# adaLN chunks with one 128-column block per column group and one transpose, and the first layer's gate chunks at the merge stage

## The chip, the core and the metric

The kernel runs on one core of one Trainium2 chip. The metric is the device time of one execution in microseconds (us).

## What is computed

One inference step of a trunk of two layers (`DEPTH` = 2), for 512 prompt positions and 8 single-position samples, 520 columns in all, with `D_MODEL` = 1024. Each layer is conditioned by adaLN: a small vector c (one row for the prompt, one for each of the 8 samples, so 9 rows) is multiplied by a 1024 x 3072 matrix, which gives shift, scale and gate. Cut to what matters:

```
mod = silu(c) @ w_ada + b_ada                  # 9 rows x 3072
shift, scale, gate = split(mod, 3)
h = rmsnorm(x) * (1 + scale) + shift           # needs shift and scale
proj = h @ w_in                                # seven projections of h
y_m = mlstm branch(proj);  y_c = convolution branch(proj)
merged = sigmoid(gm) * y_m + sigmoid(gc) * y_c
x = x + gate * (merged @ w_out)                # the gate is needed only here
```

Shift and scale are needed before the first projection of a layer, the gate only in its last product.

## The kernel before

Activations are held transposed, channels on the 128 partitions and the 520 columns along the free dimension, in tiles of 8 channel blocks (`KT` = 8). Every large product is done to nearly full float32 precision with three fast products (high x high, high x low, low x high): `split_w` loads a 128 x 1024 weight tile `raw` (L167, SP's queue), ACT rounds it to `whi` (L173), GpSimd subtracts to get `wlo` (L176), and `dense` (L188) multiplies, 48 matmuls of 128 x 260 for a block of 128 output channels. `raw` has two buffers and `whi`/`wlo` three, so the weights are prepared a few blocks ahead.

The adaLN matrix of a layer is cut into 6 chunks of 512 columns (`w_ada[l, c]`, 2 MB each in 4 transfers, L275): chunks 0 to 3 hold scale and shift, each for two channel blocks of h; chunks 4 and 5 hold the gate. One chunk goes like this. `ada_mul` (L292) multiplies the 32-column tile `cT[:, k]` (9 of its columns are c, the others zero) as weights with the chunk's 512 columns, for the 8 blocks k of the contraction. Block k writes to partitions 32(k mod 4) and up, so that four blocks in a row use the four column groups of TensorE, and the four groups hold four partial sums. ACT copies the 128 x 512 result to `asb` (L294). The `tail` (L300) then has four matmuls with 128 columns of `asb` as weights and the selector `sel32` as the other operand: this turns the block round and adds the four partial sums. DVE adds the bias into `mod` (L301), and for chunks 0 to 3 makes `sa` = (1 + scale) * norm weight (L306).

Where the chunks stand: in layer 0, chunks 0 to 3 are loaded in the prologue behind x. The first dense product is `dense_pair` (L248), a loop over the contraction that can start on the first blocks of h while the later ones are still being made: its `hook` does chunk c = 1, 2, 3 after block k = 1, 3, 5, and then makes the two blocks `hh`/`hl` of h that this chunk gives (`norm_in`, L433 to L452). After `gab(0)`, the first convolution input, come chunks 4 and 5 of layer 0, loaded into the tiles that later hold q and v; then `do_xm`, `do_v` and `do_qk` for the four heads. Layer 1's chunk 0 is loaded into the tile `xc` and multiplied in layer 0's merge stage (the loop over m that makes `mrg`, two dense products a turn) after m = 3; chunk 1 follows in the next stage; chunks 2 to 5 are done at the boundary of the layers.

The 31-tap convolution is done on DVE, tap by tap (L515), in tasks that `fill(n)` hands out between the dense products. The order of instructions on each engine is set by the framework's scheduler, which plays the program through with its own times; where an instruction stands in an engine's queue is fixed from then on. An engine that waits holds up all behind it.

Of the kernel before, what the change touches and what calls it, by code (L numbers as in the profile page):

```python
# [11 lines left out]
F32 = mybir.dt.float32  # L12
# [8 lines left out]
L = 2  # L21
D = 1024
KT = D // 128
# [52 lines left out]
def build(nc, tc, ctx, ap):  # L76
# [8 lines left out]
    sml = pool("sml")  # L85
# [3 lines left out]
    v, s, g, te = nc.vector, nc.scalar, nc.gpsimd, nc.tensor  # L89

    ident = const.tile([128, 128], F32, name="ident")
    make_identity(nc, ident)
    sel32 = const.tile([128, 32], F32, name="sel32")
# [43 lines left out]
    class Pairs:  # L137
# [7 lines left out]
        def tail(self, i, n):  # L145
            return self.tiles[i][:, :, T - n:T]

    def t520(name):
        return tmp.tile([128, T], F32, tag="t520", bufs=T5B, name=name)
# [81 lines left out]
    cT = const.tile([128, KT, 32], F32, name="cT")  # L231
# [28 lines left out]
    def ada_start(l):  # L260
        avec = sml.tile([128, 32], F32, tag="avec", bufs=2, name="avec")
        nc.sync.dma_start(avec, ap["avec"][l])
        mod = sml.tile([128, 24, 9], F32, tag="mod", bufs=2, name="mod")
        sa = sml.tile([128, KT, 9], F32, tag="sa", bufs=2, name="sa")
        return avec, mod, sa
# [11 lines left out]
    def ada_load(l, c, tag):  # L277
        raw = ada_tile(tag)
        for kp in range(0, 4, 2):
            ada_half(l, c, raw, kp)  # L280
        return raw

    def ada_chunk(l, adas, c, tag, ps=("m", 3)):
        return ada_mul(adas, c, ada_load(l, c, tag), ps)

    def ada_mul(adas, c, raw, ps=("m", 3), stream=False):
        vec, mod, sa = adas
        acc = pm("ada", *ps)
        for n in range(KT):
            k = n if stream else KT - 1 - n  # L290
            r = 32 * (k % 4)
            te.matmul(acc[r:r + 32, :], cT[:, k, :], raw[k // 2][:, k % 2, :], start=(n < 4), stop=(n >= 4))  # L292
        asb = t520("asb")
        s.copy(asb[:, 0:512], acc)  # L294

        def tail():
            pt = pm("adat", *ps)
            ks = slice(c * 4, c * 4 + 4)
            for i in range(4):
                te.matmul(pt[:, i * 9:i * 9 + 9], asb[:, i * 128:(i + 1) * 128], sel32[:, 0:9], start=True, stop=True)  # L300
            v.tensor_tensor(out=mod[:, ks, :], in0=pt[:, 0:36].rearrange("p (m r) -> p m r", r=9),  # L301
                            in1=vec[:, O_BADA + c * 4:O_BADA + c * 4 + 4].unsqueeze(2).to_broadcast([128, 4, 9]),
                            op=ALU.add)
            if c < 4:
                o = 2 * c
                v.scalar_tensor_tensor(out=sa[:, o:o + 2, :], in0=mod[:, 4 * c:4 * c + 2, :], scalar=1.0,  # L306
                                       in1=vec[:, O_NORM + o:O_NORM + o + 2].unsqueeze(2).to_broadcast([128, 2, 9]),
                                       op0=ALU.add, op1=ALU.mult)
        return tail
# [96 lines left out]
    acc = sum_sq(x)  # L406
    x_src = ap["x"]
    adas = ada_start(0)

    for l in range(L):  # L410
        avec, mod, sa = adas
# [210 lines left out]
            return proj(tuple(a[:, 512:1024] for a in w), xcs, kk, h, DH ** -0.5)  # L622

        gab(0, w=w01)
        if l == 0:
            gtails = [ada_chunk(l, adas, 4, "q"), ada_chunk(l, adas, 5, "v")]
        else:
            gtails.append(ada_mul(adas, *raws.pop(0)))
        for tail in gtails:
            tail()  # L630
        xc = big.tile([128, KT, T], F32, tag="xc", name="xc")
        q = big.tile([128, KT, T], F32, tag="q", name="q")
        kk = Pairs("k", F32, "kk")
# [2 lines left out]
        for h in range(H):  # L636
# [6 lines left out]
            mm = do_qk(h)  # L643
# [14 lines left out]
        with tc.issue_after(mm.ins):  # L658
            for r in range(6):
                for n, c in enumerate(HALF):  # L660
                    for j in range(4):
                        t, k = srcs[r * 4 + j]
                        o = O_WG + (t * 8 + k) * 8
                        te.matmul(pgs[n][32 * j:32 * j + 32, 0:HT], vec[:, o:o + 32], (q, kk, vv)[t][:, k, c],  # L664
                                  start=(r == 0), stop=(r == 5))
# [40 lines left out]
        mm = gab(2, raw=True)  # L706
        pt = pm("pst")
# [9 lines left out]
        for j in range(2):  # L717
            for h in range(H):
                te.matmul(pv_[32 * h:32 * h + 32, j * 128:(j + 1) * 128], vv[:, 2 * h + j, T - 32:T], ident,
                          start=True, stop=True)  # L720
# [4 lines left out]
        for j in range(2):  # L725
            for h in range(H):
                te.matmul(pv_[32 * h:32 * h + 32, 256:258], prod[:, 2 * h + j, :], ones[:, 0:2],
                          start=(j == 0), stop=(j == 1))
# [228 lines left out]
        mm = gab(7)  # L957
        pt = pm("pths")
# [4 lines left out]
        for j in range(2):  # L963
            v.tensor_tensor(
                out=hsm[:, :, j, :],
                in0=pt[:, j * 128:(j + 1) * 128].rearrange("p (h c) -> p h c", h=H)[:, :, S0:32],
# [6 lines left out]
        for m0 in range(0, KT, 2):  # L973
            ws = split_w(ap["wst"][l, PR_ZM + m0 // 2], 2)
            for j in range(2):
                m = m0 + j
# [31 lines left out]

        mrg = Pairs("v", F32, "mrg")
        if l + 1 < L:  # L1010
            adas = ada_start(l + 1)
            raw = ada_load(l + 1, 0, "xc")
        for m in range(KT):
            wg, wb = split_w(ap["wst"][l, PR_GMB + m], 2)
            sg = t520("sgm")
            dense(wg, hh, hl, KT, lambda c, p: s.activation(sg[:, c], p, AF.Sigmoid))

            def ev(c, p):
                i = v.tensor_tensor(out=mrg[:, m, c], in0=p, in1=sg[:, c], op=ALU.mult)
                with tc.issue_after(i.ins):  # L1020
                    fill(F_GM)

            mm = dense(wb, hmh, hml, KT, ev)
            if l + 1 < L and m == 3:
                with tc.issue_after(mm.ins):
                    tail = ada_mul(adas, 0, raw)

        sgc = Pairs("k", F32, "sgc")
        if l + 1 < L:
            tail()  # L1030
            tail = ada_chunk(l + 1, adas, 1, "q")
# [14 lines left out]
        for m0 in range(0, KT, 2):  # L1046
            ws = split_w(ap["wst"][l, PR_ZC + m0 // 2], 2)
            for j in range(2):
                m = m0 + j
# [151 lines left out]
```

## Time and profile before

| | |
|---|---|
| median of 3 runs | 1283.85 us (1280.69 to 1285.78) |
| the profiled execution | 1279.5 us, its span 1277.8 us |
| TensorE matmul (PE) busy | 1226.5 us, 96% of the span |
| VectorE (DVE), GpSimd (POOL), ScalarE (ACT) busy | 843.3, 682.4, 531.8 us |
| DMA | 177.14 MB, mean 139 GB/s |
| adaLN matmuls (L292) | 192 records for 96 matmuls, 31.0 us busy |
| tails (L300) | 96 records for 48 matmuls, 11.9 us busy |

A plain float32 matmul leaves two records in the trace (192 for 96), a transpose and a fast product one. The profile has a row for each group of instructions (line, engine, operation, tile, count), one for each stretch of the timeline, and in brackets the idle time ahead of an instruction with what ended it.

### The profile page before, as it was taken

What the parts mean: (1) busy time and instruction counts of PE and PEld (TensorE: products, weight loads), DVE (VectorE), ACT (ScalarE), POOL (GpSimd) and SP (SyncE); (2) the same over time, 40 slices, a digit from 0 to 9 for tenths busy, and PEclk for the clock granted to TensorE, in tenths of its full rate; (3) what the DMA queues carried; (4) which work ended last, traced back from release to release, by engine and by line L of the source; (5) the groups of instructions that cost most, each with busy time, mean ns of one, the idle gap of its engine ahead of it and who ended that gap; (6) DMA issues with size and microseconds to landing.
All of it is one profiled execution on the core that took longest, in us unless ns stands there. A gap on an engine that the chain in (4) does not pass through costs nothing.

```text
span 1277.8 us, 25802 instructions
## 1 busy us (share of the span) xinstructions
PE 1226.5 (96%) x10244; PEld 1155.6 (90%) x10244; DVE 843.3 (66%) x1735; ACT 531.8 (42%) x955; POOL 682.4 (53%) x899
## 2 busy tenths in 40 slices
PE   6999999999999999999999999999999999999996
PEld 3699988889999999899979997888899999989996
DVE  6495576667977993544257748666788899735424
ACT  3466554443332223532236655445434222344342
POOL 2356545556654446565635664444485545467572
PEclk9999999999999999999999999999999999999998
DMA  9632346653342342243932324566422232223322
GB/s 361 232 95 78 115 159 246 218 183 124 100 166 83 99 149 84 75 149 108 336 136 85 101 82 137 205 211 241 164 88 97 86 99 85 84 83 123 127 83 67
DMA packets 59929, 177.14 MB, mean 139 GB/s; under 512 B 13409, under 2 KB 21665, under 8 KB 55713
## 3 DMA queue, kind: packets, MB, share of 16 engines
q1 hardware_dynamic: 56928, 167.08, 38.6%
q10 hardware_dynamic: 2880, 8.42, 1.8%
q8 instruction: 80, 1.31, 0.4%
q14 instruction: 41, 0.33, 0.1%
HBM read 149.77 MB, written 25.71 MB: 137 GB/s over the span
## 4 chain that ended last, share of the span: by engine, by line
PE 80%; DVE 10%; ACT 3%; DMA 3%; POOL 2%; issue 1%; SPq 1%; DVEq 0%; ACTq 0%; POOLq 0%
PE pd L188 66%; DVE cb L780 4%; PE pds L864 3%; PE pd L248 2%; DMA o_C_p<-cf 2%; POOL wlo L176 2%; PE ada L292 1%; ACT whi L173 1%; PE pqc L768 1%; PE pcf L830 1%; DVE cv L515 1%; PE ppv L830 1%; PE pg L664 1%; DMA wada<-w_ada 1%; PE ptok L825 1%
## 5 line engine op out<-in xcount | busy, mean ns | idle before, releaser
L176 POOL TENSOR_TENSOR wlo<-raw,whi 128x256 fp32r<-128x256 f32 x680 | 523.5, 802 | 523.5 <-ACT whi L173 518.8
L188 PE MATMUL pd<-hh,whi 128*128 128x260 f32 x1728 | 495.4, 287 | 6.9 <-ACT szc L1051 5.3
L188 PE MATMUL pd<-hl,whi 128*128 128x260 f32 x1728 | 491.2, 284 | 0.0
L188 PE MATMUL pd<-hh,wlo 128*128 128x260 f32 x1728 | 490.8, 284 | 0.0
L188 PEld LDWEIGHTS pd<-hh,whi 128*128 128x128 f32 x1728 | 326.6, 189 | 14.5 <-ACT szc L1051 5.8
L188 PEld LDWEIGHTS pd<-hl,whi 128*128 128x128 f32 x1728 | 327.0, 189 | 0.4 <-issue 0.2
L188 PEld LDWEIGHTS pd<-hh,wlo 128*128 128x128 f32 x1728 | 326.8, 189 | 0.3 <-POOL wlo L176 0.2
L173 ACT CAST whi<-raw 128x1024 fp32r<-128x1024 f32 (+1 forms) x174 | 179.1, 1030 | 329.8 <-PE pd L188 276.4
L515 DVE SCALAR_TENSOR_TENSOR cv<-u,vec,cv 128x509 f32<-128x509 f32 (+6 forms) x448 | 296.5, 729 | 0.1
L780 DVE SCALAR_TENSOR_TENSOR cb<-vb,wsk,cb 128x257 f32<-128x257 f32 x128 | 72.7, 616 | 4.0 <-POOL cb L777 4.0
L188 PE MATMUL pd<-hmh,whi 128*128 128x260 f32 x256 | 72.4, 283 | 0.0
L188 PE MATMUL pd<-hml,whi 128*128 128x260 f32 x256 | 72.4, 283 | 0.0
L188 PE MATMUL pd<-hmh,wlo 128*128 128x260 f32 x256 | 72.3, 283 | 0.0
L188 PE MATMUL pd<-zl,whi 128*128 128x260 f32 x256 | 72.0, 283 | 0.0
L188 PE MATMUL pd<-zh,wlo 128*128 128x260 f32 x256 | 72.0, 283 | 0.0
L188 PE MATMUL pd<-zh,whi 128*128 128x260 f32 x256 | 71.8, 283 | 0.0
L188 PE MATMUL pd<-ml,whi 128*128 128x260 f32 x224 | 63.3, 283 | 0.0
L188 PE MATMUL pd<-mh,whi 128*128 128x260 f32 x224 | 63.3, 283 | 0.0
L188 PE MATMUL pd<-mh,wlo 128*128 128x260 f32 x224 | 63.2, 283 | 0.0
L324 DVE SCALAR_TENSOR_TENSOR xr<-pd,mod,xo 128x260 f32<-128x260 f32 (+1 forms) x32 | 15.3, 484 | 61.7 <-PE pd L188 38.9
L777 POOL TENSOR_SCALAR cb<-cb,bc 128x514 f32<-128x514 f32 x64 | 51.5, 825 | 1.3 <-PE pqc L768 1.3
L188 PE MATMUL pd<-xcs,whi 128*128 128x260 f32 x256 | 47.9, 287 | 3.0 <-ACT vv L568 2.9
(306 smaller groups left out, 2251.3 us busy)
## 6 DMA issues: line engine op xcount, KB each, us to landing
raw<-wst SPq DMA_DIRECT2D x160, 512.0 KB, 3.8
wada<-w_ada SPq DMA_DIRECT2D x36, 512.0 KB, 8.1
cb<-C SPq DMA_DIRECT2D x16, 1028.0 KB, 6.5
o_C_s<-cb SPq DMA_DIRECT2D x16, 1028.0 KB, 5.4
vb<-vsc SPq DMA_DIRECT2D x16, 514.0 KB, 5.5
wada<-w_ada ACTq DMA_DIRECT2D x12, 512.0 KB, 5.8
raw<-wqkv SPq DMA_DIRECT2D x8, 512.0 KB, 3.5
x<-x SPq DMA_DIRECT2D x4, 520.0 KB, 7.0
```

What stands on the lines that cost most here:

```text
L173: s.copy(hi, sl)
L176: g.tensor_tensor(out=lo[:, cs], in0=sl[:, cs], in1=hi.bitcast(F32)[:, cs], op=ALU.subtract)
L188: mm = te.matmul(p[:, 0:HT], a[:, ws], b[:, k, HALF[c]], start=(n == 0), stop=(n == 3 * nk - 1))
L248: te.matmul(p[:, 0:HT], a[:, ws], b[:, k, HALF[c]], start=(k == 0 and i == 0), stop=(k == KT - 1 and i == 2))
L292: te.matmul(acc[r:r + 32, :], cT[:, k, :], raw[k // 2][:, k % 2, :], start=(n < 4), stop=(n >= 4))
L324: v.scalar_tensor_tensor(out=x[:, m, c.start:c.start + n], in0=p[:, 0:n], scalar=mod[:, 16 + m, 0:1], in1=xo[:, c.start:c.start + n], op0= ...
L515: v.scalar_tensor_tensor(out=acc[a][:, sft:TP], in0=u[:, k, 0:TP - sft], scalar=wcol(sft), in1=acc[a][:, sft:TP], op0=ALU.mult, op1=ALU.add)
L664: te.matmul(pgs[n][32 * j:32 * j + 32, 0:HT], vec[:, o:o + 32], (q, kk, vv)[t][:, k, c], start=(r == 0), stop=(r == 5))
L777: g.tensor_scalar(out=cb[:, 2 * h:2 * h + 2, :], in0=cb[:, 2 * h:2 * h + 2, :], scalar1=bc[:, 0, h, b:b + 1], scalar2=1.0, op0=ALU.mult, o ...
L780: v.scalar_tensor_tensor(out=cb[:, 2 * h + j, :], in0=vb[:, h, :], scalar=wsk[:, h, j, b:b + 1], in1=cb[:, 2 * h + j, :], op0=ALU.mult, op ...
L830: te.matmul(p, a, b, start=(first and n == 0), stop=(last and n == 2))
L864: te.matmul(p[:, 0:n], kk[:, 2 * h + j, t0:t0 + 128], q[:, 2 * h + j, t0:TP], start=(j == 0), stop=(j == 1))
```

## The change

In `ada_mul` each block k is now multiplied by four matmuls of 128 columns, one for each column group, and each column group sums over all 8 blocks by itself: 32 matmuls of 32 x 128 instead of 8 of 32 x 512. The result is 128 x 128 and already summed, so ACT copies a quarter of the columns, and one transpose takes the place of the four matmuls with the selector. `asb` gets two small buffers of its own. In the code's order the two gate chunks of layer 0 leave their place after `gab(0)`; they are loaded one after the other into `xc` in the merge stage and multiplied after m = 1 and m = 3, and layer 1's chunk 0 after m = 5 instead of m = 3. The tails of the two gate chunks follow at once.

```diff
         for n in range(KT):
             k = n if stream else KT - 1 - n
-            r = 32 * (k % 4)
-            te.matmul(acc[r:r + 32, :], cT[:, k, :], raw[k // 2][:, k % 2, :], start=(n < 4), stop=(n >= 4))
-        asb = t520("asb")
-        s.copy(asb[:, 0:512], acc)
+            for j in range(4):
+                mm = te.matmul(acc[32 * j:32 * j + 32, 0:128], cT[:, k, :],
+                               raw[k // 2][:, k % 2, j * 128:(j + 1) * 128], start=(n == 0), stop=(n == KT - 1))
+        asb = sml.tile([128, 128], F32, tag="asb", bufs=2, name="asb")
+        s.copy(asb, acc[:, 0:128])
 
         def tail():
             pt = pm("adat", *ps)
             ks = slice(c * 4, c * 4 + 4)
-            for i in range(4):
-                te.matmul(pt[:, i * 9:i * 9 + 9], asb[:, i * 128:(i + 1) * 128], sel32[:, 0:9], start=True, stop=True)
-            v.tensor_tensor(out=mod[:, ks, :], in0=pt[:, 0:36].rearrange("p (m r) -> p m r", r=9),
+            te.transpose(pt[:, 0:128], asb, ident)
+            v.tensor_tensor(out=mod[:, ks, :], in0=pt[:, 0:128].rearrange("p (m r) -> p m r", r=32)[:, :, 0:9],
...
         gab(0, w=w01)
-        if l == 0:
-            gtails = [ada_chunk(l, adas, 4, "q"), ada_chunk(l, adas, 5, "v")]
-        else:
+        if l:
             gtails.append(ada_mul(adas, *raws.pop(0)))
-        for tail in gtails:
-            tail()
+            for tail in gtails:
+                tail()
...
         if l + 1 < L:
+            late = adas
             adas = ada_start(l + 1)
-            raw = ada_load(l + 1, 0, "xc")
+            turns = [(late, l, 4), (late, l, 5), (adas, l + 1, 0)]
+            raw = ada_load(*turns[0][1:], "xc")
         for m in range(KT):
...
             mm = dense(wb, hmh, hml, KT, ev)
-            if l + 1 < L and m == 3:
+            if l + 1 < L and m % 2 == 1 and turns:
+                who, _, c = turns.pop(0)
                 with tc.issue_after(mm.ins):
-                    tail = ada_mul(adas, 0, raw)
+                    tail = ada_mul(who, c, raw)
+                if turns:
+                    raw = ada_load(*turns[0][1:], "xc")
+                    tail()
```

What this moves is seen at three places. The first is TensorE in layer 0's `dense_pair`, at the end of chunk 3 (`ada` is the chunk's product, `adat` its tail, `pd` at L248 is `dense_pair`). Before:

```order
L292 MATMUL ada<-wada,cT 32x512 x2
L300 MATMUL adat<-sel_83,asb 128x9 x4
L248 MATMUL pd<-hh,whi 128x260 x2
L292 MATMUL ada<-wada,cT 32x512
L248 MATMUL pd<-hl,whi 128x260
L248 MATMUL pd<-hh,wlo 128x260
L248 MATMUL pd<-hh,whi 128x260
L248 MATMUL pd<-hl,whi 128x260
L248 MATMUL pd<-hh,wlo 128x260
L248 MATMUL pd<-hh,whi 128x260
L292 MATMUL ada<-wada,cT 32x512 x7
```

And now, at the same tail of chunk 3 (`pd` at L188 is `do_xm(0)`, the dense product that follows `dense_pair` in the code):

```order
L248 MATMUL pd<-hh,whi 128x260
L248 MATMUL pd<-hl,whi 128x260
L248 MATMUL pd<-hh,wlo 128x260
L300 MATMUL adat<-ident,asb 128x128
L188 MATMUL pd<-hh,whi 128x260
L188 MATMUL pd<-hl,whi 128x260
L248 MATMUL pd<-hh,whi 128x260 x2
L188 MATMUL pd<-hh,wlo 128x260
L188 MATMUL pd<-hh,whi 128x260
L188 MATMUL pd<-hl,whi 128x260
```

Chunk 4, which stood as one and seven matmuls inside `dense_pair`, is gone from here, the tail is one row, and matmuls of the next product are mixed in behind it. Over the whole of `dense_pair`, chunks 1, 2 and 3 stand in pieces of 8, 8, 16 and 16, 8, 8 and 24, 8 small matmuls between the dense ones, where before they stood in 2, 2, 4 and 6, 2 and 2, 2, 2, 2; 14 dense products stand between the last piece of chunk 3 and its tail, and in the merge stage 22 between a gate chunk and its tail. The second place is ACT's queue around the same tail (`asb` is the copy of chunk 3, `whi` a weight tile for `do_xm(0)`, `hh` the last two blocks of h). Before:

```order
L294 COPY asb<-ada 128x512
L433 ACTIVATE hh<-x,mod,sa 128x512 x2
L318 CAST hh<-hs 128x2x8
L173 CAST whi<-raw 128x1024
L533 COPY sg<-pd 128x260 x2
```

And now:

```order
L295 COPY asb<-ada 128x128
L173 CAST whi<-raw 128x1024
L433 ACTIVATE hh<-x,mod,sa 128x512 x2
L318 CAST hh<-hs 128x2x8
L533 COPY sg<-pd 128x260
```

The rounding of that weight tile has moved ahead of the last two blocks of h. The third place is SP's queue in layer 0's merge stage (each turn m loads two weight tiles `raw`; the numbers tell them apart). Before, from m = 1 on:

```order
L167 DMA raw_4546<-wst 128x1024
L167 DMA raw_4555<-wst 128x1024
L275 DMA wada_4404<-w_ada 128x1024 x4
L167 DMA raw_4689<-wst 128x1024
L167 DMA raw_4698<-wst 128x1024
```

And now, from m = 1 on:

```order
L167 DMA raw_4583<-wst 128x1024
L167 DMA raw_4592<-wst 128x1024
L275 DMA wada_4441<-w_ada 128x1024 x4
L167 DMA raw_4769<-wst 128x1024
L167 DMA raw_4778<-wst 128x1024
L167 DMA raw_4906<-wst 128x1024
L167 DMA raw_4915<-wst 128x1024
L275 DMA wada_4761<-w_ada 128x1024 x4
L167 DMA raw_5086<-wst 128x1024
L167 DMA raw_5095<-wst 128x1024
```

The first load stands where it stood, and two more (only the first of them is shown) stand behind the weights of m = 3 and of m = 5, ahead of those of m = 4 and m = 6.

## The prediction

> **What bounds the kernel now.** First the page: is one engine busy all the time?
>
> ```profile
> PE 1226.5 (96%) x10244; PEld 1155.6 (90%) x10244; DVE 843.3 (66%) x1735; ACT 531.8 (42%) x955; POOL 682.4 (53%) x899
> ...
> PE   6999999999999999999999999999999999999996
> ...
> DMA  9632346653342342243932324566422232223322
> ```
>
> TensorE works in every slice; it idles 1277.8 - 1226.5 = 51.3 us in all. So TensorE time that goes is mostly time gained, and TensorE time added is lost, unless a stretch has another limit. The stretches that the change touches:
>
> ```profile
> 30.00:40.00 10.00, 10.00 (x61) 5.78 (x58) 4.51 (x15) 3.05 (x6) 0.00 (x0) 1.00 1.02 367
> 40.00:50.00 10.00, 7.97 (x54) 4.56 (x52) 2.84 (x9) 3.26 (x5) 1.71 (x3) 1.00 0.76 294
> 60.00:70.00 10.00, 10.00 (x85) 10.00 (x86) 10.00 (x19) 5.21 (x12) 5.02 (x9) 1.00 0.34 106
> 400.00:440.00 40.00, 40.00 (x337) 38.43 (x336) 32.70 (x56) 8.91 (x13) 18.91 (x27) 1.00 0.26 85
> ```
>
> Columns: length, busy PE, weight loads, DVE, ACT, POOL, granted clock, DMA share, GB/s. At 30 to 40 us (`dense_pair`, layer 0) TensorE is full with 61 records and the DMA engines are full too; at 60 to 70 it is full with 85, and so is DVE; the merge stage (400 to 440) is full on TensorE alone. So 61 records in 10 us is slow work, not much work. TensorE's list of waits says whether data are late there:
>
> ```profile
> PE ada L292 <- DMA wada<-w_ada: 1.2, 2, 1.0
> ```
>
> Two waits for chunk data, 1.2 us in all. The front is bound by TensorE's order and by the chain chunk, copy, tail, h.
>
> **Chunks 1 to 5 in the front.** L292's records alone, one stretch for each chunk:
>
> ```profile
> 19.00:26.00 7.00, 3.17 (x16) 0.47 (x16) 0.42 (x1) 1.00 1.02 407
> 28.00:32.00 4.00, 2.96 (x16) 0.54 (x16) 0.00 (x1) 1.00 1.01 407
> 33.00:43.10 10.10, 4.21 (x16) 0.58 (x16) 0.03 (x1) 1.00 1.01 354
> 46.00:50.40 4.40, 2.96 (x16) 0.54 (x16) 0.00 (x0) 1.00 0.35 142
> 57.00:60.00 3.00, 1.92 (x16) 0.42 (x16) 0.48 (x1) 1.00 0.75 175
> ```
>
> The same 16 records cost 1.92 us in one piece and 4.21 when cut into four pieces: a piece of two matmuls uses two of the four column groups. After the change each block k fills all four groups by itself, so a cut costs only the run-out. The nearest rows for the new form are the column sums of the layer norm (weights of 32 columns, four column groups, 130 columns each), beside a chunk in one piece:
>
> ```profile
> 403.65 1.92 PE L292 MATMUL ada<-wada,cT 128*32 128x512 f32 x16
> 405.51 0.39 PE L188 MATMUL pd<-hh,whi 128*128 128x260 f32 x1
> ...
> 477.41 1.76 PE L195 MATMUL lnm<-u,ones 128*32 128x130 f32 x56
> 479.10 0.39 PE L188 MATMUL pd<-hh,whi 128*128 128x260 f32 x1
> ...
> L195 PEld LDWEIGHTS lnm<-u,ones 128*32 128x32 f32 x128 | 3.3, 109 | 0.6
> ```
>
> From start to the next product, 1.86 us for the old chunk; 1.69 us for seven k (56 records), so 0.24 a k and 1.93 a chunk now. In one piece nothing is gained. In pieces it is: chunks 1 to 3 have 3 + 3 + 2 = 8 pieces in the new order, 24 x 0.24 + 8 x 0.2 (run-out, an estimate between none and the 0.27 of a record) = 7.4 instead of 3.17 + 2.96 + 4.21 = 10.3: **2.9 us gained**. Bounds: 1.7 with 0.27 and 0.27 a k, 4.6 with no run-out.
>
> **The tails.** Four selector matmuls (eight records) between dense products, and one transpose between them:
>
> ```profile
> 670.01 0.29 PE L248 MATMUL pd<-hh,wlo 128*128 128x260 f32 x1
> 670.14 0.95 PE L300 MATMUL adat<-sel,asb 128*128 128x9 f32 x8
> 670.95 0.37 PE L248 MATMUL pd<-hl,whi 128*128 128x260 f32 x1
> 671.15 0.28 PE L248 MATMUL pd<-hh,wlo 128*128 128x260 f32 x1
> ...
> 312.41 0.29 PE L188 MATMUL pd<-hl,whi 128*128 128x260 f32 x1
> 312.54 0.27 PE L919 MATMUL pth<-ident,q 128*128 128x128 f32 x1
> 312.57 0.37 PE L188 MATMUL pd<-hh,wlo 128*128 128x260 f32 x1
> 312.78 0.28 PE L188 MATMUL pd<-hh,whi 128*128 128x260 f32 x1
> ```
>
> Two steps of dense products take 0.24 us. With the old tail between them 671.15 - 670.01 = 1.14, so it costs 0.90; with a transpose 0.37, so 0.13. A tail saves 0.77. For chunks 1 to 3: **2.3 us**. By the Trainium skill (TensorE: Matmul & The Clock Gate, Part 4) a transpose takes about 275 ns in a kernel; the record's 0.27 agrees, and were all of it on the path, twelve would cost 1.7 us more; the rows show half of it hidden.
>
> The copy in front of the tail shrinks:
>
> ```profile
> L294 ACT COPY asb<-ada 128x512 f32<-128x512 f32 x12 | 7.0, 586 | 26.3 <-PE ada L292 26.3
> ...
> L867 ACT ACTIVATE dd<-pu,stT 128x128 f32<-128x128 f32 x8 | 3.0, 369 | 0.8 <-PE pu L862 0.5 <-ACT Ph L871 0.2
> ```
>
> No copy of 128 x 128 is in the trace; the 369 ns of an activation of that size from PSUM is taken (0.2 less), with no saving and 0.45 as bounds. How much of it counts is seen at chunk 3:
>
> ```profile
> 41.97 1.05 PE L292 MATMUL ada<-wada,cT 128*32 128x512 f32 x4
> 43.07 0.59 ACT L294 COPY asb<-ada 128x512 f32<-128x512 f32 x1 [6.88 <-PE ada L292]
> 43.71 1.06 PE L300 MATMUL adat<-sel,asb 128*128 128x9 f32 x8 [0.69 <-ACT asb L294]
> 45.25 1.52 ACT L433 ACTIVATE hh<-x,mod,sa 128x512 fp32r<-128x512 f32 x2 [1.59 <-DVE sa L306]
> 46.12 0.51 PE L248 MATMUL pd<-hh,whi 128*128 128x260 f32 x2 [1.35 <-ACT hh L433]
> ```
>
> TensorE waits 0.69 for the copy and 1.35 for h, and DVE, which needs the tail's result for `sa`, has nothing else. In the new order the copy of chunk 3 is covered by fourteen dense products, but chunk 2's stands bare, and h of chunk 3 is still waited for, with two matmuls of `do_xm(0)` as cover. I count **0.3 us** less idle (bounds 0 and 1.5).
>
> Chunks 4 and 5 go from here: 2.96 + 1.92, and two tails of 0.90: **6.7 us**. Their eight transfers also leave SP's queue and the DMA engines; as nothing waited for data by then, nothing is counted for that.
>
> Front: 2.9 + 2.3 + 0.3 + 6.7 = **12.2 us**.
>
> **The merge stage** takes both chunks back, on a full TensorE: 2 x (1.93 + 0.16 + 0.13) = **4.4 us** added. The 0.16 is for the change of column layout and back (the step 670.95 to 671.15 is 0.20 where others are 0.12, on each side); the 0.13 is the transpose. The copies and the bias adds lie beside dense products, the tail stands some 22 matmuls behind its chunk. The two new loads wait on SP for the product ahead of them, and the weights of m = 4 and m = 6 queue behind; I cost this at nothing, since the weights' buffers are free only about then too.
>
> **Layer 1.** Tails of chunks 0 and 1, between dense products: 2 x 0.77 = 1.5 us. At the boundary:
>
> ```profile
> 649.50 3.62 PE L292 MATMUL ada<-wada,cT 128*32 128x512 f32 x32
> 652.94 0.41 PE L195 MATMUL rmsn<-sqo,ones 128*32 128x130 f32 x8
> 653.27 1.95 PE L300 MATMUL adat<-sel,asb 128*128 128x9 f32 x16
> 657.46 1.13 PE L203 MATMUL rb<-yi,ident 128*128 128x130 f32 x8 [0.38 <-DVE yi L160]
> ```
>
> The last column sum stands behind two chunks, and DVE's chain to `rb` (L203) starts with it, so 4.5 us from one to the other whatever the tails cost. In the new order it stands behind one chunk and half of the next: 1.5 x 1.93 = 2.9 instead of 3.44, **0.5 us** earlier. The tails of chunks 2 to 4 lie beside that chain or beside DVE's work on h, and are counted at nothing; chunk 5's lies between dense products, 0.77. Layer 1 in all: **2.8 us** (bounds 1.5 and 5).
>
> **Sum:** 12.2 - 4.4 + 2.8 = 10.6 us. The profiled execution took 1279.5 (its span 1277.8), so 1268.9; it was 0.34% below the median of 1283.85, and in that measure the forecast is **1273.2**. With the terms' bounds the gain is 7 to 16 us.
>
> **Rivals.**
>
> *DVE sets the end of the front.* The convolution starts when `u` is made, and then DVE has no gap:
>
> ```profile
> 55.22 0.76 DVE L540 TENSOR_TENSOR u<-pd,sg 128x260 f32<-128x260 f32 x2 [7.51 <-ACT sg L535]
> ...
> 91.01 0.68 DVE L523 TENSOR_TENSOR u<-cv,co 128x511 f32<-128x511 f32 x1
> 92.87 1.31 DVE L618 TENSOR_TENSOR xcs<-xc,xcs 128x520 fp32r<-128x520 f32 x2 [1.18 <-ACT xcs L617]
> ```
>
> 36 us of work. `u` comes about 6 us earlier (5.5 for `dense_pair`; its sigmoid now stands behind one more weight tile and the first `xm` copies), while TensorE wants to be 12 us earlier by then. If the projections wait for DVE, the front gives 6: gain 6 - 4.4 + 2.8 = 4.4, **1279**. Against it: in the new order the two `xms` and the taps for `do_xm(0)` stand further ahead on DVE. 15%.
>
> *Data or a weight tile come late in the front.* ACT now rounds a weight tile ahead of the last blocks of h; and DMA is full to 40 us, so chunk 3 may not be there when TensorE is ready for it, some 3 us sooner than before. Then the 5.5 us of chunks 1 to 3 are lost and only 6.7 - 4.4 + 2.8 = 5.1 remain: **1279** again. Against it: 1.2 us of waits for chunk data so far. 10%.
>
> *Slower: the weight loads are not hidden.* A k has eight loads where two were, each 109 ns. In series that is 0.87 us a k and 7.0 a chunk instead of 1.93: 12 x 5.1 = 61 us more, **1334**. It would turn the sign from 10.6 / 96 k = 0.11 us a k, that is, one load of eight. For it speaks nothing in the trace; against it speak the 56 loads of `lnm` in 1.76 us. The Trainium skill (TensorE: Matmul & The Clock Gate, Part 3, what overlaps) says that a load overlaps running matmuls only when its row group differs; here all loads use the same full rows. By that rule the loads would stand in series, and the `lnm` rows contradict it. 4%, with whatever else makes it slower.
>
> *The order elsewhere is dealt anew and takes back or adds a few us.* Outside the front, the merge stage and the boundary the queues hold nearly the same rows. 5%, half of it on either side.
>
> **How the numbers follow.** The forecast has 66%, 7 to 16 us of gain, 1268 to 1277. The two rivals at 1279 have 25% and lie just inside 0.5% of no change (6.4 us, about what a measurement can tell here). The range is 1267 to 1281: both, and the bounds. Faster by over 0.5%: 66 plus a part of the rivals where they strike half, 74%; same 20%; slower 6%.
>
> **What would show it.** Chunks 1 to 3 at 2.2 to 2.7 us each of L292, one in the merge stage at 1.9 to 2.1; tails as single records of 0.27; the first `do_v` product some 11 to 12 us earlier than now, layer 0's merge stage ending 7 to 8 earlier, the end 10. Wrong, if TensorE shows waits for `xms`, `xcs` or `hh` of several us before 110 us (the first two rivals), or if chunks take over 3 us in one piece.

## The result, and the profile after

| | before | after |
|---|---|---|
| median | 1284.82 us (4 runs, 1280.69 to 1286.39) | 1271.7 us (4 runs, 1268.9 to 1272.92) |
| the profiled execution, its span | 1279.5 us, 1277.8 us | 1268.9 us, 1267.2 us |
| TensorE busy, idle in the span | 1226.5 us, 51.3 us | 1215.3 us, 51.9 us |

The ratio of the times is 0.9903, with a 95% interval of 0.988 to 0.9926: about 12 us faster (9.5 to 15.4). 1273.2 was forecast for the median and 1268.9 for the profiled execution. The total is that of the forecast; whether its parts are is the question of what follows. First the page of after, its first line and TensorE's row of slices:

```profile
PE 1215.3 (96%) x10736; PEld 1163.3 (92%) x10736; DVE 841.2 (66%) x1735; ACT 527.4 (42%) x955; POOL 680.4 (54%) x899
...
PE   6999989999999999999999998999999999999996
```

TensorE is the bound as before, and its busy time fell by 1226.5 - 1215.3 = 11.2 us, while its idle time stayed nearly the same. The groups of the chunk, its copy and its tail in after (operation, shapes, count, busy us, mean ns, idle time ahead):

```profile
L292 PE MATMUL ada<-wada,cT 128*32 128x128 f32 x768 | 26.4, 284 | 3.5 <-DMA wada<-w_ada 3.4
L300 PE MATMUL adat<-ident,asb 128*128 128x128 f32 x12 | 3.5, 291 | 0.8 <-ACT asb L295 0.7
L295 ACT COPY asb<-ada 128x128 f32<-128x128 f32 x12 | 3.2, 264 | 23.9 <-PE ada L292 23.9
```

The waits for chunk data grew from 1.2 to 3.4 us. The longest is at the start of chunk 1, first of before, then of after:

```profile
19.82 1.05 PE L292 MATMUL ada<-wada,cT 128*32 128x512 f32 x4 [0.98 <-DMA wada<-w_ada]
...
19.53 0.64 PE L292 MATMUL ada<-wada,cT 128*32 128x128 f32 x16 [2.73 <-DMA wada<-w_ada]
```

The data are there no later than before (19.53 against 19.82 us); TensorE is ready for them sooner. The longer wait by itself loses nothing against before, but what chunk 0 and its tail gained ahead of it is gone. L292 alone, in the stretches that hold chunks 1, 2 and 3 of layer 0, and then the three turns of the merge stage (length, busy PE and weight loads, clock, DMA share, GB/s):

```profile
19.00:26.00 7.00, 2.77 (x64) 1.81 (x64) 0.76 1.03 417
26.90:33.00 6.10, 2.37 (x64) 1.56 (x64) 1.00 1.02 391
33.40:38.00 4.60, 2.16 (x64) 1.63 (x64) 1.00 0.71 232
368.00:372.00 4.00, 1.95 (x64) 1.69 (x64) 1.00 0.47 142
394.00:397.00 3.00, 1.96 (x64) 1.69 (x64) 1.00 0.43 158
419.00:422.00 3.00, 1.95 (x64) 1.69 (x64) 1.00 0.46 164
```

The three chunks in pieces take 2.77 + 2.37 + 2.16 = 7.30 us (7.4 forecast), one in a piece 1.95 (1.93 forecast). Chunk 1 ran in a stretch where the granted clock was 0.76 in the mean, and one of its pieces took 1.05 us where a piece of that size takes 0.64 at full clock: 0.4 of the 7.30.

Where the time came from is read at instructions that stand in both traces. Of before: the first copy of a `do_v` product (L568), the first `pst`, the last sigmoid of the merge stage, `pst` of layer 1, the wait for `szc` of layer 1, and the last normalisation:

```profile
80.83 0.67 ACT L568 COPY vv<-pd 128x260 f32<-128x260 f32 x2
177.96 0.62 PE L710 MATMUL pst<-ident,sxt 128*128 128x128 f32 x2 [2.98 <-DVE sxt L688]
446.88 0.38 ACT L1016 ACTIVATE sgm<-pd 128x260 f32<-128x260 f32 x1
797.06 0.41 PE L710 MATMUL pst<-ident,sxt 128*128 128x128 f32 x2 [2.95 <-DVE sxt L688]
1131.42 0.39 PE L188 MATMUL pd<-hh,whi 128*128 128x260 f32 x1 [2.67 <-ACT szc L1051]
1269.57 0.52 PE L363 MATMUL frb<-yi,ident 128*128 128x65 f32 x3 [3.04 <-DVE yi L160]
```

The same in after, with the last column sum of the boundary (`rmsn`, 652.94 in before) as well:

```profile
69.51 0.67 ACT L568 COPY vv<-pd 128x260 f32<-128x260 f32 x2
165.60 0.41 PE L708 MATMUL pst<-ident,sxt 128*128 128x128 f32 x2 [2.98 <-DVE sxt L686]
439.99 0.38 ACT L1016 ACTIVATE sgm<-pd 128x260 f32<-128x260 f32 x1
639.95 0.41 PE L195 MATMUL rmsn<-sqo,ones 128*32 128x130 f32 x8
783.93 0.41 PE L708 MATMUL pst<-ident,sxt 128*128 128x128 f32 x2 [2.97 <-DVE sxt L686]
1119.45 0.39 PE L188 MATMUL pd<-hh,whi 128*128 128x260 f32 x1 [2.67 <-ACT szc L1055]
1258.40 0.45 PE L363 MATMUL frb<-yi,ident 128*128 128x65 f32 x1 [3.04 <-DVE yi L160]
```

By subtraction, after is ahead by 11.3 us at `do_v`, 12.4 at `pst`, 6.9 at the end of the merge stage, 13.0 at the boundary, 13.1 at layer 1's `pst`, 12.0 at its `szc` and 11.2 at the end. Between the merge stage and the boundary 6.1 us are gained, and the forecast had 2.0 there (two tails, 1.5, and 0.5 at the boundary). Most of the rest is at one place. Before, in the stage behind `layer_norm`: the sums on POOL, `szc` on ACT, the next product on TensorE, and a window from there:

```profile
513.40 2.65 POOL L224 TENSOR_TENSOR total<-total,lsq 128x520 f32<-128x520 f32 x2
514.72 0.67 ACT L1051 ACTIVATE szc<-pd 128x260 f32<-128x260 f32 x2 [1.78 <-POOL total L224]
515.16 0.39 PE L188 MATMUL pd<-hh,whi 128*128 128x260 f32 x1 [2.67 <-ACT szc L1051]
...
516.00:519.00 3.00, 3.00 (x16) 3.00 (x15) 0.00 (x0) 0.39 (x1) 0.06 (x1) 0.50 0.04 15
```

And after:

```profile
504.72 0.67 ACT L1055 ACTIVATE szc<-pd 128x260 f32<-128x260 f32 x2
505.16 0.39 PE L188 MATMUL pd<-hh,whi 128*128 128x260 f32 x1 [0.39 <-ACT szc L1055]
...
513.00:517.00 4.00, 4.00 (x46) 3.80 (x38) 3.22 (x10) 1.34 (x2) 1.15 (x2) 1.00 0.43 131
```

TensorE waited 2.67 us for `szc`, and ran at half clock behind it (16 records in 3 us). Now it waits 0.39, and the clock stays at 1.00. `szc` and the squares `lsq` ahead of it take buffers from the ring of four `t520`, where before `asb` had one from its copy to its tail behind `layer_norm`. In the trace of after five squares are made before POOL adds the second one, in before four. That is theory C of the experiments: the small buffer for `asb`, a side edit of the change, gave what the prediction had not seen. In layer 1, where no `asb` stands at this place, the wait of 2.67 us is in both kernels (the rows at 1131.42 and 1119.45 above): POOL takes the first square there only behind a weight tile, so the ring is full after four squares all the same.

### The profile page after: what moved, and what is told of

Same layout as the page of the kernel before. It is cut to its first block, busy times and chain, and to the rows that moved or that the text cites. A ratio compares the mean times of both kernels' runs of the same rounds, so it can differ in the third digit from the quotient of the medians.

```text
span 1267.2 us, 26766 instructions
## 1 busy us (share of the span) xinstructions
PE 1215.3 (96%) x10736; PEld 1163.3 (92%) x10736; DVE 841.2 (66%) x1735; ACT 527.4 (42%) x955; POOL 680.4 (54%) x899
## 4 chain that ended last, share of the span: by engine, by line
PE 77%; DVE 9%; DMA 5%; ACT 3%; issue 3%; POOL 2%; SPq 0%; DVEq 0%; ACTq 0%; POOLq 0%
PE pd L188 65%; DVE cb L778 4%; PE pds L862 2%; DMA o_C_p<-cf 2%; POOL wlo L176 2%; PE pcf L828 1%; PE pqc L766 1%; PE ada L292 1%; ACT whi L173 1%; PE pd L248 1%; DMA raw<-wst 1%; PE pg L662 1%; DMA wada<-w_ada 1%; DVE bst L795 1%; PE ppv L828 1%
## 5 line engine op out<-in xcount | busy, mean ns | idle before, releaser
L188 PE MATMUL pd<-hh,whi 128*128 128x260 f32 x1728 | 496.7, 288 | 5.0 <-ACT szc L1055 3.8
L188 PE MATMUL pd<-hl,whi 128*128 128x260 f32 x1728 | 492.2, 285 | 0.0
L188 PE MATMUL pd<-hh,wlo 128*128 128x260 f32 x1728 | 492.0, 285 | 0.0
L188 PEld LDWEIGHTS pd<-hh,whi 128*128 128x128 f32 x1728 | 327.8, 190 | 11.3 <-ACT szc L1055 4.4
L188 PEld LDWEIGHTS pd<-hh,wlo 128*128 128x128 f32 x1728 | 328.0, 190 | 0.7 <-issue 0.4
L188 PEld LDWEIGHTS pd<-hl,whi 128*128 128x128 f32 x1728 | 327.9, 190 | 0.6 <-issue 0.4
L188 PE MATMUL pd<-hmh,whi 128*128 128x260 f32 x256 | 72.5, 283 | 0.0
L188 PE MATMUL pd<-hml,whi 128*128 128x260 f32 x256 | 72.5, 283 | 0.0
L188 PE MATMUL pd<-hmh,wlo 128*128 128x260 f32 x256 | 72.4, 283 | 0.0
L188 PE MATMUL pd<-zl,whi 128*128 128x260 f32 x256 | 71.8, 282 | 0.0
L188 PE MATMUL pd<-zh,wlo 128*128 128x260 f32 x256 | 71.8, 282 | 0.0
L188 PE MATMUL pd<-zh,whi 128*128 128x260 f32 x256 | 71.6, 282 | 0.0
L188 PE MATMUL pd<-mh,whi 128*128 128x260 f32 x224 | 63.1, 283 | 0.0
L188 PE MATMUL pd<-mh,wlo 128*128 128x260 f32 x224 | 63.1, 282 | 0.0
L188 PE MATMUL pd<-ml,whi 128*128 128x260 f32 x224 | 63.1, 282 | 0.0
L775 POOL TENSOR_SCALAR cb<-cb,bc 128x514 f32<-128x514 f32 x64 | 51.3, 822 | 1.3 <-PE pqc L766 1.3
L188 PE MATMUL pd<-xcs,whi 128*128 128x260 f32 x256 | 47.8, 287 | 2.3 <-ACT vv L568 2.0
```

The source lines that it names most:

```text
L188: mm = te.matmul(p[:, 0:HT], a[:, ws], b[:, k, HALF[c]], start=(n == 0), stop=(n == 3 * nk - 1))
L775: g.tensor_scalar(out=cb[:, 2 * h:2 * h + 2, :], in0=cb[:, 2 * h:2 * h + 2, :], scalar1=bc[:, 0, h, b:b + 1], scalar2=1.0, op0=ALU.mult, o ...
```

## The experiments

The theories: A, the prediction's terms add up. B, the move of the gate chunks is what pays. C, the ring. D, a stretch of half clock follows a long wait of TensorE, so such a wait costs more than its length. Each experiment was timed beside the kernel before; the medians are in the text of each.

**1. Only the new form.** The kernel before with the new `ada_mul` and its tail; the gate chunks stay behind `gab(0)`.

> The kernel before with only the new form of a chunk (one block per column group, one transpose, small asb); the gate chunks stay in the front. Theory A (the terms of the prediction add up; the form is nearly all of it): front 2.9 + 2.3 + 0.3, chunk 4 shorter by 1.0, two more tails 1.5, layer 1 2.8 = 10.8 us less than before, so within 1 us of the changed kernel. Theory B (the move is what pays): some 5 us less than before. Theory C (the wait for szc in layer 0 went because asb left the ring of four t520 buffers, 2.3 us and a dip of the granted clock of 1.5): that wait of 2.67 us is gone here too.

Measured: 1277.91 us, ratio 0.9951 (0.9933 to 0.9969), 5.5 us less than before by the medians; theory A missed by half. The wait for `szc` of 2.67 us is gone in layer 0, as C says. The rest is small because the front falls short: at the first `do_v` copy (77.69) this run is 3.1 us ahead of before, where the terms have 2.9 + 2.3 + 0.3 + 1.0 + 1.5 = 8.0. Windows, and two rows of TensorE (chunk 3's tail, and the product behind chunk 4):

```profile
15.40:18.80 3.40, 3.26 (x25) 2.46 (x25) 1.08 (x3) 1.21 (x2) 1.04 (x2) 0.50 1.02 407
22.20:29.00 6.80, 6.03 (x50) 5.32 (x51) 6.05 (x17) 0.47 (x2) 2.53 (x3) 0.50 1.02 413
...
42.26 0.27 PE L300 MATMUL adat<-ident,asb 128*128 128x128 f32 x1
...
50.41 0.39 PE L188 MATMUL pd<-hh,whi 128*128 128x260 f32 x1 [0.87 <-ACT whi L173]
```

10.2 us at half clock, where before has none in the front; chunk 3's tail comes at 42.26, 1.5 us earlier than before and 2.9 later than in after; and a wait for a weight tile is new. How the 4.9 us divide among these is not shown (see experiment 9).

**2. Only the move.** The changed kernel with the old `ada_mul`, tail and `asb`.

> The changed kernel with the old form of a chunk (8 matmuls of 512 columns, copy of 128x512, four selector matmuls, asb in the t520 ring); only the move of the gate chunks is left. Theory A: front 6.7 less, merge stage 2 x (1.86 + 0.16 + 0.90) = 5.8 more: 0.9 us less than before, no difference that can be measured. Theory B (the move pays): 5 us less. Theory C: the wait of 2.67 us for szc in layer 0 is there as before, with a clock dip behind it.

Measured: 1282.85 us, ratio 0.9995 (0.998 to 1.001): no difference, as A says, and against B. In its trace the merge stage pays two chunks as expected, and of the front's gain a part is taken back by waits for `xms` (1.40, 0.55 and 1.80 us at 71 to 76 us) and a stretch of half clock at 73.30 to 80.10. That is the first rival in small. `szc` waits 2.66, as C says.

Form and move do not simply add up: 0.9951 and 0.9995 make 0.9946, and the changed kernel is at 0.9903, some 5.5 us less (by the three intervals, 1 to 10). The half clock in experiment 1's front and the waits for `xms` in this one's are what the traces show of it.

**3. `asb` in the ring again.** The changed kernel with one line of before:

```diff
-        asb = sml.tile([128, 128], F32, tag="asb", bufs=2, name="asb")
+        asb = t520("asb")[:, 0:128]
```

> The changed kernel, asb taken from the ring of t520 buffers again; nothing else. Theory A: no difference to the changed kernel (under 1 us). Theory C (a copy of a chunk that waits for its tail holds one of the four buffers): TensorE waits some 2.7 us for szc in layer 0 where the changed kernel waits 0.39, and with a dip of the granted clock behind it the run is 2 to 4 us longer than the changed kernel.

Measured: 1275.9 us, ratio 0.9937 (0.9914 to 0.9961), 4.2 us above the changed kernel's median (the two intervals overlap slightly; 2 to 4 expected by C). POOL, ACT, TensorE and the window of this run:

```profile
510.83 2.65 POOL L224 TENSOR_TENSOR total<-total,lsq 128x520 f32<-128x520 f32 x2
...
512.14 0.67 ACT L1055 ACTIVATE szc<-pd 128x260 f32<-128x260 f32 x2 [1.78 <-POOL total L224]
512.58 0.39 PE L188 MATMUL pd<-hh,whi 128*128 128x260 f32 x1 [2.66 <-ACT szc L1055]
...
513.00:517.00 4.00, 4.00 (x23) 4.00 (x22) 0.00 (x0) 0.39 (x1) 0.48 (x1) 0.57 0.17 64
```

The picture of before is back in every row, from one line. C holds for this wait, and the chunks alone (theory A) are worth 1283.43 - 1275.9 = 7.5 us here (5.0 to 11.0), not 10.6. The 4.2 us are not all shown to be this wait: in the two traces this run is 1.4 us behind the changed kernel at the first `pst`, 5.0 at the start of the merge stage and at its end, and 7.4 behind the wait for `szc` (512.58 against 505.16). So 2.4 us are lost at the wait. Between the first two points no chunk stands; what the traces show there is 3.4 us more of half clock and 1.6 us more of waits for the tile `dd`.

**4. A tail of four matmuls.** The changed kernel, in the tail:

```diff
-            te.transpose(pt[:, 0:128], asb, ident)
+            for i in range(4):
+                te.matmul(pt[:, i * 9:i * 9 + 9], asb, ident[:, 32 * i:32 * i + 9], start=True, stop=True)
```

> The changed kernel, the transpose of each tail replaced by four matmuls (eight records) with asb as weights and 9 columns of the identity; the chunk's products stay. Theory A (a tail costs 0.77 us more on the path wherever TensorE is full): 3 in the front, 2 in the merge stage, 2 in the next stage, 1 in layer 1's first dense products, 8 x 0.77 = 6.2 us longer than the changed kernel. Rival (TensorE waits for h behind the tails in the front anyway, so these are hidden): 3 to 4 us longer.

Measured: 1278.33 us, 0.995 (0.9932 to 0.9968), 6.6 us above the changed kernel's median, 6.2 expected. The time by itself does not exclude the rival's 3 to 4 (the two intervals reach 2 to 3 us to either side), but the traces settle the term: from the product ahead of a tail to the second behind it, this run takes 1.13 us at each of the tails at 380.72, 406.59, 452.75 and 664.11, the changed kernel 0.35 at 373.59, 398.87, 444.60 and 651.79. That is 0.78 a tail, and 0.77 was forecast.

**5. Work ahead of `pst`.** 24 spare products in each layer, in front of the wait of 2.98 us.

> The changed kernel with 24 spare dense products (2.9 us, their result is not used) in TensorE's queue shortly ahead of the transposes pst of each layer, where TensorE waits 2.98 us for sxt. Theory D (a stretch of half clock follows a wait of TensorE of some 2.7 us or more; in the traces of before, of the changed kernel and of the first four runs nearly every dip begins within 2.5 us of the end of such a wait): both dips behind pst go, some 1.5 us for each 3.4 us of half clock where dense products follow, less where they do not: 1 to 4 us shorter than the changed kernel, though TensorE does more. Rival (the dips come by themselves, or the wait is too short for them): the dips stay and the run is as long as the changed kernel or up to 1 us longer.

Measured: 1278.16 us, 0.9953 (0.9935 to 0.9972), 6.5 longer than the changed kernel. It could not test D, since the wait did not fill, it moved:

```profile
168.38 0.63 PE L712 MATMUL pst<-ident,sxt 128*128 128x128 f32 x4 [3.01 <-DVE sxt L686]
```

The spare work stands on TensorE ahead of products whose result DVE takes before it makes `sxt`. Work is put into a wait only if it stands behind everything that the wait's end needs.

**6. `szc` in another ring.** The changed kernel:

```diff
-                sz = t520("szc")
+                sz = s8.tile([128, T], F32, tag="s8", bufs=S8B, name="szc")
```

> The changed kernel, szc taken from the three buffers of the ring s8, which are free in this stage, instead of the t520 ring. Theory C (ring): the waits for szc, 2.67 us in layer 1 and 0.39 + 0.75 in layer 0, go, and with them the dip of the clock behind the one in layer 1 (1.5 us): 3 to 5 us shorter than the changed kernel. Rival (the wait is for the psum buffer or for POOL's sums, and only changes its name): within 1 us.

Measured: 1287.81 us, 1.0034 (1.0021 to 1.0047), 16 us longer than the changed kernel. Both expectations miss. ACT and TensorE in layer 0, then TensorE in layer 1:

```profile
525.72 5.06 ACT L1005 ACTIVATE u<-u,vec 128x520 f32<-128x520 f32 x8 [1.51 <-DVE u L1003]
530.69 0.61 ACT L318 CAST zh<-u 128x520 fp32r<-128x520 f32 x1
531.20 0.64 ACT L1055 ACTIVATE szc<-pd 128x260 f32<-128x260 f32 x2
531.62 0.59 PE L188 MATMUL pd<-hh,whi 128*128 128x260 f32 x1 [5.63 <-ACT szc L1055]
...
1156.62 0.58 PE L188 MATMUL pd<-hh,whi 128*128 128x260 f32 x1 [8.87 <-ACT szc L1055]
```

Three buffers are too few: a `szc` is held until `u` comes out of `layer_norm`, the fourth finds no buffer, and it stands on ACT behind all of `u` (six halves, three blocks, are done before, the next at 531.20). So the number of free buffers decides, more than which ring they are from (experiments 10 and 12).

**7. Column group by column group.** The changed kernel, in the chunks with `stream=False`: all 8 blocks k of one column group, then the next group.

```diff
-        for n in range(KT):
+        for i in range(4 * KT):
+            n, j = (i // 4, i % 4) if stream else (i % KT, i // KT)
             k = n if stream else KT - 1 - n
-            for j in range(4):
```

> The changed kernel; in the eight chunks that are not in the front (chunks 4 and 5 of layer 0, all six of layer 1) the 32 matmuls stand column group by column group, 8 blocks k each, instead of block by block with four groups each. Theory A (0.24 us a block because four column groups run at once): one at a time a pass of 128 columns takes a quarter of the 0.427 us that a pass of 512 columns took in the trace of before, 8 passes a block 0.85 us, a chunk 6.8 instead of 1.95: 4.9 us more for each of the 8, of which those in waits are partly hidden: 25 to 39 us longer. Rival (the weight loads set the pace, 64 a chunk in either order): no difference.

Measured: 1303.1 us in a single run, 31 us longer than the changed kernel, within the 25 to 39 expected. One chunk in the merge stage, first of this run, then of the changed kernel:

```profile
L292 PE MATMUL ada<-wada,cT 128*32 128x128 f32 x64 | 6.0, 274 | 0.0
```

```profile
L292 PE MATMUL ada<-wada,cT 128*32 128x128 f32 x64 | 2.0, 274 | 0.0
```

The same 64 records with the same mean duration (274 ns) take 6.0 us instead of 2.0. What makes a chunk cheap is that neighbours in the queue write to different column groups. The rival, that the number of loads sets the pace, falls: it is the same in both orders. Whether the loads or the products of one group stand in line is not shown.

**8. Work in the front's wait.** Three spare float32 matmuls (2.84 us) behind chunk 0's tail in the changed kernel.

> The changed kernel with three spare float32 matmuls of 128x512 (2.6 us) in TensorE's queue behind chunk 0's tail, where it waits 2.73 us for chunk 1's data. Theory D: the dip of the clock in the front (3.4 us at half clock, about 1 us of loss) goes: 0.5 to 1.5 us shorter than the changed kernel. Rival (the front is bound by its data, the clock costs nothing there): no difference, or the spare work delays chunk 1 and it is up to 1 us longer.

Measured: 1272.12 us, 0.9906 (0.9884 to 0.9928): no difference to the changed kernel. The wait for chunk 1's data and the half clock behind it are gone from the front (mean granted clock 1.00 over the first 160 us, 0.99 in after), but the front is no shorter: the first `do_v` copy starts at 69.33 against 69.51. The spare work itself holds up chunk 1, which starts at 20.70 instead of 19.53.

**9. The same spare work, the form only.** The three matmuls in the kernel of experiment 1:

> The kernel of the first run (only the new form of a chunk) with the three spare float32 matmuls behind chunk 0's tail. Its front had two stretches of half clock (10.2 us in all) that the kernel before has not, and chunk 3's tail came 2.9 us later than in the changed kernel. Theory D: these stretches go and the run is 2 to 3 us shorter than the first run, so some 8 us shorter than before. Rival (the front is bound by its data; the first run is slower than its terms for another reason): no difference to the first run.

Measured: 1276.12 us, 0.9935 (0.9914 to 0.9956), 1.8 us below experiment 1, less than the 2 to 3 of D and within the intervals. The two stretches at 15 to 29 us are gone, another came at 42.1. At the first `do_v` copy (76.23) it is 4.6 us ahead of before, experiment 1 was 3.1, and the terms have 8.0: so the two stretches are not all that the front of experiment 1 falls short. Undecided by time; in the traces the stretches went with the wait, both times.

**10. `szc` in wide tiles.** The changed kernel with room for all eight blocks of `szc`:

```diff
-                sz = t520("szc")
+                if m % 4 == 0:
+                    szs = s8.tile([128, 4, T], F32, tag="s8", bufs=S8B, name="szc")
+                sz = szs[:, m % 4]
```

> The changed kernel, szc in two wide tiles of four blocks each from the ring s8, so that no szc waits for a buffer (in the run with one block a buffer, three buffers were too few: szc waited behind u on ACT). Theory C in its amended form (TensorE is held where szc finds no free buffer, or stands on ACT behind work that finds none): the waits for szc of 2.67 us in layer 1 and of 0.39 and 0.75 in layer 0 go, with the dip behind the first: 3 to 5 us shorter than the changed kernel. Rival (what stands ahead of szc in ACT's queue decides, and the order is dealt anew): a wait for szc of over 2 us stays in one of the layers, at another place, and the run is within 2 us of the changed kernel or longer.

Measured: 1269.24 us, 0.9882 (0.9861 to 0.9903), the shortest of all, 2.5 us below the changed kernel by the medians (3 to 5 expected; the intervals overlap). The window over layer 1's stage, first of this run, then of the changed kernel:

```profile
1100.00:1140.00 40.00, 40.00 (x350) 39.32 (x349) 9.12 (x29) 16.45 (x29) 28.04 (x35) 1.00 0.27 81
```

```profile
1100.00:1140.00 40.00, 37.33 (x310) 36.78 (x309) 17.58 (x45) 18.31 (x31) 23.68 (x28) 0.96 0.24 80
```

TensorE no longer idles there, the clock stays at 1.00, and 40 records more are done in the same 40 us.

**11. Spare work inside the wait for `sxt`,** five matmuls that read `u`:

> The changed kernel with five spare float32 matmuls of 128x260 (2.1 us) behind gab(2), reading its result u, so that they stand in the wait for sxt and not ahead of work that the chain to sxt needs (24 spare products ahead of it only moved the wait and cost 3.0 us a layer). Theory D: the wait of 2.98 us falls to about 1, the dips behind pst go in both layers, 1 to 3 us shorter than the changed kernel. Rival (dips do not come from this wait): they stay, no difference.

Measured: 1278.27 us, 0.9948 (0.9927 to 0.9969), 6.6 longer than the changed kernel. The spare work itself waited 2.56 us, for a later write of DVE to that part of `u`. Like experiment 5 it says nothing on D.

**12. The edit of experiment 10 in the kernel before,** to price `szc` without the chunks:

> The kernel before with szc in two wide tiles from the ring s8, the chunks untouched. It prices the waits for szc apart from the chunks: by theory C the wait of 2.67 us goes in both layers (5.3 us), and with it the stretch of half clock that mostly follows (1.5 us each): 4 to 8 us less than before. If the four-buffer ring was not what held TensorE there: under 2 us.

Measured: 1275.87 us, 0.9923 (0.9911 to 0.9935), 10 us less than the 1286.01 of before beside it, more than the 4 to 8 expected. The stage of each layer, first of the kernel before, then of this run:

```profile
505.00:545.00 40.00, 37.33 (x309) 36.78 (x308) 20.25 (x39) 19.71 (x35) 24.07 (x28) 0.96 0.24 75
1110.00:1150.00 40.00, 37.33 (x321) 36.78 (x321) 16.93 (x45) 18.03 (x31) 24.18 (x30) 1.00 0.24 79
```

```profile
505.00:545.00 40.00, 40.00 (x347) 39.66 (x346) 18.05 (x38) 22.21 (x38) 26.19 (x30) 1.00 0.27 87
1110.00:1150.00 40.00, 40.00 (x346) 39.66 (x345) 13.31 (x39) 18.01 (x31) 26.28 (x33) 1.00 0.27 89
```

Against this kernel, that of experiment 10 is the change of the chunks alone, with no wait for `szc` on either side: 0.9882 / 0.9923 = 0.9959, 5 us (2.2 to 8.4 by the two intervals). By experiment 3 it was 7.5. In the traces of the two the lead is 8.3 us at the last `yc` of layer 0 (601.14 against 592.89) and 5.5 at the last normalisation (1263.20 against 1257.68); experiment 10 has 3.4 us more of half clock between.

## Why the prediction was right, step by step

**The total was right, but a term of some 4 us was missing under it.** 10.6 us were forecast from the chunks alone. By the runs that have `szc` alike on both sides, the chunks gave 5 (experiment 10 against 12) to 7.5 (experiment 3 against before). Read by place in the two traces, up to the boundary of the layers, they gave 11.6 - 4.7 + 2.3 = 9.2 of the 9.8 forecast there, and `szc`, which no term had, gave 3.8: 13.0 in all, which agrees with the medians.

That the profiled execution came to 1268.9, as forecast to the digit, is luck. The profiled execution of before had a mean granted clock of 0.993, above all of the 20 runs beside experiments 1 to 4 (0.985 to 0.992); that of after had 0.989, as its other runs (0.988 to 0.989). Between the boundary and the end after loses 13.0 - 11.2 = 1.8 us, and has 6.8 us more of half clock there, ahead of the last stage.

- **Chunks 1 to 3:** right. 7.30 us against 7.4. At full clock a piece of two blocks takes 0.64 us, of four 1.08, of six 1.52: 0.22 a block and a run-out of 0.2. That the sum with 0.24 a block fits so closely is owed to the 0.4 of half clock.
- **Tails:** right. Single records of 0.27, and 0.78 a tail by the rows of experiment 4 against 0.77. The copy took 264 ns, not the 369 that stood for it.
- **Idle in the front:** right at chunk 3, wrong in sign over the front. Two rows of TensorE at chunk 3 in after:

```profile
39.39 0.28 PE L300 MATMUL adat<-ident,asb 128*128 128x128 f32 x1
...
41.43 0.51 PE L248 MATMUL pd<-hh,whi 128*128 128x260 f32 x2 [1.52 <-ACT hh L433]
```

  At chunk 3 the waits fell from 0.69 + 1.35 to 1.52 us, and chunk 2's copy stands bare for 0.44, as the prediction said. But the wait for chunk 1's data is 2.73 instead of 0.98, with a stretch of half clock behind it. The tail comes 43.71 - 39.39 = 4.3 us earlier, with 72 dense products ahead of it in both traces; pieces and two tails make 2.9 + 1.5 = 4.4. This is not the second rival: chunk 3 was not late, and chunk 1's data came no later than before. Behind h the lead is 4.9 us (46.12 against 41.43, with two products more done by then), of 5.5 forecast. Where chunks 4 and 5 had stood it grows to 11.3 at `do_v` and 12.4 at `pst`, so the front came to its 12.2.
- **Merge stage:** mis-sized by little. 11.6 us ahead at its start by the products that stand in both traces, 6.9 at its end: 4.7 against 4.4.
- **Layer 1:** the two tails and the boundary came as forecast (6.1 us between merge stage and boundary, less 3.8 for `szc`, is 2.3 against 2.0). Chunk 5's tail (0.77) was gained but not kept: counted by the same dense products, after is 13.3 us ahead in front of it and 14.1 behind it. Then TensorE waits 0.39 and 1.75 us for `xms`, where before waited 1.76 once, and at layer 1's `pst` 13.1 are left. The prediction had no such wait in its sum.
- **Not in the sum at all:** `szc` (2.3 us of wait and some 1.5 of clock gained at its place), and the granted clock. In the profiled pair after lost more to it than before: four stretches of half clock ahead of the last stage, 17 us long in all, against three with 10.2. In the timed runs the mean clock of the two is the same, 0.988.
- **DVE as the bound of the front** (15%): not in the changed kernel, where `xms` cost TensorE 3.7 us in both layers together against 2.8; in experiment 2, with the old form, it took back a part of the front. **Weight loads** (4%): they did not stand in series. 64 loads of 110 ns, 7.0 us in series, take 1.95 with their products in the merge stage, and experiment 7 says what that hangs on. The rule of the Trainium skill that the prediction cites for this rival does not hold here, where neighbours write to different column groups.

What stays open: why the chunks are worth 9.2 us by place but 5 to 7.5 by those runs (their intervals reach from 2 to 11), and which part of that goes to the clock and which to waits; experiments 5, 8, 9 and 11 were to tell of the clock and did not.

## What to carry to other kernels

When a change takes a temporary out of a shared ring of buffers, list who else takes buffers from that ring and who waits on the engine behind them: here this was some 4 of the 12 us. A total that fits says little on its parts; undo them one by one, the side edits too. A longer wait is not lost time by itself: look when it ends. The small matmuls of a chunk are cheap here when neighbours in the queue go to different column groups, and three times as dear when they do not.

## What the runs showed of the hardware

After the first 10 us and ahead of the last stage, the granted clock falls to half in stretches of 3.4, 6.8 or 10.2 us, and in these traces that goes with TensorE's waits. In the 14 profiles, of the waits of over 3.2 us 4 of 4 have such a stretch beginning in or within 2.2 us behind them; of those of 2.8 to 3.2 us 28 of 28; of 2.6 to 2.8 us 12 of 17; of 2 to 2.6 us 4 of 5; of 1.5 to 2 us 8 of 22; of 1 to 1.5 us 5 of 26. Dense products of before inside such a stretch:

```profile
516.22 0.42 PE L188 MATMUL pd<-hl,whi 128*128 128x260 f32 x1
516.44 0.42 PE L188 MATMUL pd<-hh,wlo 128*128 128x260 f32 x1
```

A step is 0.22 us instead of 0.12, so 3.4 us of it cost about 1.5. By this estimate a wait of TensorE of nearly 3 us costs about half as much again; no run changed such a wait alone and measured that. The times go with the clock: the 20 runs of before beside experiments 1 to 4 lie between a mean clock of 0.985 (1289.82 us) and 0.992 (1278.62), with scatter. By the Trainium skill (TensorE: Matmul & The Clock Gate, Part 1) the gate closes after an idle window of about 3.4 us, with windows that run freely. The lengths here are multiples of 3.4, but waits of 2.98 and 2.67 us were enough.

A block of a chunk, four float32 matmuls of 128 columns with 32-column weights on the same rows (eight loads and eight matmul records), takes 0.24 us (1.95 / 8) in four column groups, and 0.75 (6.0 / 8) in one.
